# Where two kinds of weights wait: pooled weights two to a raw tile, and the last gate rows in two half-size tiles

## The chip, the cores and the metric

The kernel runs on one core of a Trainium2 chip. The metric is the time of one execution on the device in microseconds (us); a run's time is given as the median over repeated executions. Five engines work side by side: TensorE (PE in the profile; its weight loads are listed as PEld), VectorE (DVE), ScalarE (ACT), GpSimd (POOL) and SyncE (SP). In this kernel GpSimd does next to nothing, and SyncE only issues DMA transfers.

## The reference

The reference is one layer of an encoder block over 1024 tokens of width 1024 in float32: a SwiGLU feed-forward part, a mixing part, a second SwiGLU part and a final norm. The mixing part is where the change lies:

```python
q, k, v, g_ret, p, gates = split(u @ w_in)
ret = retention(rotary(q), rotary(k), v)          # 4 heads of 256
ret = per_head_rms(ret) * silu(g_ret)
pool_out = multiscale_pool(p, pool_w, pool_scale) # 4 groups: (mean - token) @ pool_w[g]
gate = sigmoid(gates + gate_bias)                 # two branches
merged = gate[0] * (ret @ w_ret_up) + gate[1] * (pool_out @ w_pool_up)
h = h + merged @ w_out
```

Each of the four pooling groups has a matrix `pool_w[g]` of 256x256. `w_pool_up` is 1024x1024.

## The kernel before, in words

Activations lie transposed: 128 features on the partitions, 1024 tokens along the row, so a matrix of 1024x1024 is eight tiles. Every float32 operand of a matmul is split into a high part (ScalarE's cast, line 161) and a low part (VectorE's subtraction, line 162; lines 165 and 166 for a split that also scales), and each product takes three matmuls: high by high, high by low, low by high (lines 181 to 183, and 711 to 714 in the plain products). Most large products use Strassen's scheme with seven products of half-size blocks; the products of the pooled branch are plain.

The work is a list of steps, each a preparation (loads, combinations and splits of weights) and a body (the matmuls and what follows them). `Flow.run` issues the preparation of a step four steps ahead of its body, and after each body a few items of background work. This source order is a priority: the framework that builds the program places each instruction as its operands and tiles become free, so the order on an engine can differ from the source's. Instructions under `soon()` get a high priority. SyncE issues its DMAs strictly in the order so found: one that waits holds up those behind it.

The tiles in on-chip memory come from pools by tag:

- `raw`: 4 tiles of 128x1024 float32 (4 KB on each partition, 512 KB in all), for weights as they come from memory, and for some rows.
- `c2`: 8 tiles of 128x512, for combinations of weight blocks (`ru0S` and so on), differences, and sums on their way.
- `wt`: 5 tiles that hold split weights; `mv`: 28 tiles for split activations and some rows; `tl` (4) and `t4` (9) for other rows.

A tile is free for its next user when its last reader is done; if that reader is a store, when the store has landed.

The sequence around the change, in the source's order:

1. The projections' last groups, g2 and g3, use the raw tiles in pairs (`ra`, `rb`).
2. The retention: eight units, and between their steps the pooled branch as filler. First `pool(n)` for the four groups (lines 1379 to 1405): it loads the group's pooled rows (`pl`, two raw tiles for groups 2 and 3; those of groups 0 and 1 have other tiles), loads the block `pool_w[n]` of 128x512 into the first half of a raw tile (`pw`), and splits it. Its products `px` are scaled and split into `po`, which become operands of the next part.
3. `pool_up` (lines 1407 to 1423): for each of the eight tiles mt, the weights `pu0raw` to `pu7raw` (one raw tile each), split in two parts, and the gate rows `pg` (one raw tile each, loaded from `gates`). When the products `pu0d` to `pu7d` are done, VectorE multiplies them onto the gate rows (line 1419), and the result is stored from the same raw tile to `pm`.
4. The merge: groups `ru0` to `ru3` (Strassen groups, prepared two by two), whose weights come in two raw tiles each, `ru0ra`, `ru0rb`, `ru1ra`, `ru1rb` and so on. `combine` (line 455) forms S1 and S2 from them in c2 tiles, line 468 forms S3 in place, line 472 S4. Their results are multiplied by gate rows `rg` (line 1749) and added to the stored `pm` rows (line 1750). Then come the groups `wo0` to `wo3` of the output projection.

So four raw tiles are passed on from `pl` and `pw` to `pu` and `pg` and then to `ru`. All DMAs named here are issued by SyncE (line 140, the helper `load`).

Of the kernel before, what the change touches and what calls it, by code (L numbers as in the profile page):

```python
# [15 lines left out]
ADD, SUB, MUL = ALU.add, ALU.subtract, ALU.mult  # L16
# [4 lines left out]
KT = D // P  # L21
# [69 lines left out]
def block_kernel(ctx: ExitStack, tc, x, x_tok, vecs, f1_in, f1_out, w_in, w_v, pool_w, w_ret, w_pool, w_o,  # L91
# [3 lines left out]
    tt = nc.vector.tensor_tensor  # L95
# [12 lines left out]
    def mv(name):  # L108
        return sb.tile([P, 2, H], F32R, tag="mv", bufs=N_MV, name=name)

    def wt(name, at=0):

        w = sb.tile([P, S + LINE], F32R, tag="wt", bufs=N_WT, name=name)
        return w[:, at : at + S].rearrange("p (z i c) -> p z i c", z=2, i=4)
# [5 lines left out]
    def raw(name):  # L120
        return sb.tile([P, S], F32, tag="raw", bufs=N_RAW, name=name)
# [7 lines left out]
    def c2(name):  # L129
        return sb.tile([P, H], F32, tag="c2", bufs=N_C2, name=name)  # L130
# [8 lines left out]
    def load(dst, src):  # L139
        nc.sync.dma_start(dst, src)  # L140
# [5 lines left out]
    def spill(name, n, width=S):  # L146
        return [dr.tile([P, width], F32, tag=f"{name}{i}", name=f"{name}{i}") for i in range(n)]

    def half(t, j):
        return t[:, j * H : (j + 1) * H]  # L150
# [6 lines left out]
    def flat(w, j, n=4):  # L157
        return w[:, j, :n].rearrange("p a b -> p (a b)")

    def split(hi, lo, src):  # L160
        copy(hi, src)  # L161
        tt(lo, src, hi.bitcast(F32), SUB)  # L162

    def split_scaled(hi, lo, src, by):
        act(hi, src, AF.Copy, scale=by)
        stt(lo, src, by, hi.bitcast(F32), MUL, SUB)

    def operand(src, name):
        m = mv(name)
        split(m[:, 0], m[:, 1], src)  # L170
        return m

    def weights(src, name, at=0):
        w = wt(name, at)
        n = src.shape[-1] // P
        split(flat(w, 0, n), flat(w, 1, n), src)
        return w

    def mm3(dst, w, m, start, stop):

        mm(dst, w[0], m[0], start=start, stop=False, skip_group_check=True)  # L181
        mm(dst, w[0], m[1], start=False, stop=False, skip_group_check=True)  # L182
        mm(dst, w[1], m[0], start=False, stop=stop, skip_group_check=True)  # L183

    def parts(m, at=slice(None)):
        return m[:, 0, at], m[:, 1, at]
# [503 lines left out]
    def plain(M, nk, src, name, evac, begin, banks):  # L690

        t = {}
        for q in range(0, nk, 4):

            def prep(q=q):
                if q == 0:
                    t["raw"] = raw(f"{name}raw")
                    load(t["raw"][:, : nk * P], src)
                t[q] = weights(t["raw"][:, q * P : (q + 4) * P], f"{name}w{q}")
                if q + 4 == nk:  # L700
                    begin()

            def body(q=q):
                if q == 0:
                    t["dst"] = [f(f"{name}d{j}") for j, f in enumerate(banks)]
                for i in range(4):
                    w = parts(t[q], i)
                    m = [parts(M(q + i)[j]) for j in range(2)]
                    first, final = q + i == 0, q + i == nk - 1
                    for j in range(2):  # L710
                        mm(t["dst"][j], w[0], m[j][0], start=first, stop=False)
                        mm(t["dst"][j], w[0], m[j][1], start=False, stop=False)
                    for j in range(2):
                        mm(t["dst"][j], w[1], m[j][0], start=False, stop=final)
                if q + 4 == nk:
                    evac(t["dst"])

            yield prep, body
# [396 lines left out]
    gates = spill("gt", 2 * KT)  # L1115
    pm, ret = spill("pm", KT), spill("ret", KT)
# [16 lines left out]
    def await_stored(*names):  # L1133
        flow.until(lambda: stored.issuperset(names))
# [236 lines left out]
    def pooled_rows(n, i, first=False):  # L1371

        await_stored(f"p{n}")
        name = f"pl{n}{i}"
        r = wide(name) if first else raw(name)
        load(r, pooled[2 * n + i])
        early[n, i] = [operand(half(r, j), f"{name}{j}") for j in range(2)]

    def pool(n):
        Mg, w = {}, []  # L1380

        def prep():
            for i in range(2):
                if (n, i) not in early:
                    pooled_rows(n, i)
                Mg[i] = early[n, i]
            r = raw(f"pw{n}")
            load(half(r, 0), pool_w[n])
            w.append(weights(half(r, 0), f"pw{n}"))

        def body():
            for i in range(2):
                mt = 2 * n + i
                dst = [f(f"px{mt}{j}") for j, f in enumerate((sum_bank, bank))]
                for kt in range(2):
                    for j in range(2):
                        mm3(dst[j], parts(w[0], 2 * kt + i), parts(Mg[kt][j]), kt == 0, kt == 1)
                M[mt] = []
                for j in range(2):
                    m = mv(f"po{mt}{j}")  # L1400
                    with soon():
                        split_scaled(m[:, 0], m[:, 1], dst[j], vec[:, V_SCALE + mt : V_SCALE + mt + 1])
                    M[mt].append(m)

        return prep, body

    def pool_up():
        gate = {}
        for mt in range(KT):

            def begin(mt=mt):
                gate[mt] = raw(f"pg{mt}")
                await_stored(f"t{(KT + mt) // 2}")
                load(gate[mt], gates[KT + mt])

            def evac(dst, mt=mt):
                gt = gate.pop(mt)
                for j in range(2):
                    tt(half(gt, j), dst[j], half(gt, j), MUL)
                load(pm[mt], gt)  # L1420

            yield from plain(M.get, KT, w_pool[mt], f"pu{mt}", evac, begin,
                             (sum_bank, sum_bank if mt < 4 else bank))

    def fillers():

        for n in range(4):
            yield pool(n)
        yield from pool_up()
# [560 lines left out]
```

## Time and profile before

| what | value |
|---|---|
| median of 3 runs | 2144.27 us (2141.74 to 2145.18) |
| the profiled execution's own time | 2143.71 us |
| its span, first to last instruction | 2141.8 us |
| granted TensorE clock, mean | 1.000 |
| moved by DMA | 313.59 MB, mean 146 GB/s |
| the four loads of `pw` (256 KB each) | 2.6 / 3.5 / 4.7 us to landing (least, median, most) |
| the eight loads and eight stores of `pg` (512 KB each) | 2.6 / 3.7 / 6.8 us to landing |

How to read it: every instruction has its line in the kernel, engine, operation, and the tiles that it writes and reads, without buffer numbers (`pg<-pu7d,pg` writes pg from pu7d and pg). A bracket `[1.94 <-DVE ru1wS L162]` says that the engine stood idle for 1.94 us before the instruction, and what ended the wait. In a row of windows stand the stretch, its length, then for PE, PEld, DVE, ACT and POOL the busy time with the number of instructions, the granted clock, the DMA engines' busy share, and GB/s. Matmuls overlap: one takes 0.39 us and the next begins 0.23 us later.

### The profile page before, as it was taken

Reading aid. Unit: us, or ns where it says so; the run is one execution under the profiler, and the core shown is the slowest. Engines: PE = TensorE matmul, PEld = TensorE weight load, DVE = VectorE, ACT = ScalarE, POOL = GpSimd, SP = SyncE. Lnnn points to the kernel's source line nnn. Section 1 sums busy time; section 2 is a strip of 40 time slices with the busy share of each in tenths; the row PEclk is TensorE's granted clock in tenths of the full one; section 3 lists DMA queues with packets and bytes.
Section 4 is the critical chain, followed back from the end, with each engine's and each line's share of the span. In section 5 each row is a group of like instructions: output and inputs, shape, how many; then the busy total and the mean of one; then the engine's idle time right before and its main releaser. Section 6 shows DMA issues by size and latency. Waiting matters only on the chain.

```text
span 2141.8 us, 30121 instructions
## 1 busy us (share of the span) xinstructions
PE 2129.9 (99%) x10798; PEld 1809.6 (84%) x10798; DVE 1874.0 (87%) x3352; ACT 1103.3 (52%) x2082; POOL 0.2 (0%) x4
## 2 busy tenths in 40 slices
PE   9999999999999999999999999999999999999998
PEld 7888888888888888888888998788888888888887
DVE  8798898997986799999988888899988978899796
ACT  8544444554644544544457753456644544455454
POOL 0000000000000000000000000000000000000000
PEclk9999999999999999999999999999999999999999
DMA  7232323585543333233336567624133232358542
GB/s 259 75 133 74 138 84 130 200 275 178 173 142 94 109 121 115 106 122 109 119 128 227 196 203 262 220 89 163 64 105 117 90 123 84 131 199 275 192 138 99
DMA packets 116101, 313.59 MB, mean 146 GB/s; under 512 B 12784, under 2 KB 17008, under 8 KB 115952
## 3 DMA queue, kind: packets, MB, share of 16 engines
q1 hardware_dynamic: 115376, 310.63, 42.6%
q8 instruction: 84, 1.38, 0.3%
q10 hardware_dynamic: 576, 1.05, 0.1%
q14 instruction: 65, 0.53, 0.1%
HBM read 220.93 MB, written 90.70 MB: 145 GB/s over the span
## 4 chain that ended last, share of the span: by engine, by line
PE 91%; DVE 6%; DMA 1%; ACT 1%; issue 1%; SPq 0%; ACTq 0%; DVEq 0%
PE a_b L181 2%; PE a_b L182 2%; PE a_b L183 2%; PE c_b L181 2%; PE c_b L182 2%; PE c_b L183 2%; PE c_e L182 2%; PE c_e L181 2%; PE c_e L183 2%; PE a_e L181 2%; PE a_e L182 2%; PE a_e L183 2%; PE a_a L181 1%; PE a_a L183 1%; PE a_a L182 1%; PE c_a L181 1%
## 5 line engine op out<-in xcount | busy, mean ns | idle before, releaser
L182 PE MATMUL c_b<-n3T,c_wS 128*128 128x512 f32 x176 | 68.6, 390 | 0.0
L183 PE MATMUL c_b<-n3T,c_wS 128*128 128x512 f32 x176 | 68.5, 389 | 0.0
L181 PE MATMUL c_b<-n3T,c_wS 128*128 128x512 f32 x176 | 68.4, 390 | 0.0
L182 PE MATMUL a_b<-n1T,a_wS 128*128 128x512 f32 x168 | 65.4, 389 | 0.0
L181 PE MATMUL a_b<-n1T,a_wS 128*128 128x512 f32 x168 | 65.4, 389 | 0.0
L183 PE MATMUL a_b<-n1T,a_wS 128*128 128x512 f32 x168 | 65.3, 389 | 0.0
L181 PE MATMUL a_a<-n1R,a_wL 128*128 128x512 f32 x120 | 46.7, 389 | 0.0
L182 PE MATMUL a_a<-n1R,a_wL 128*128 128x512 f32 x120 | 46.7, 389 | 0.0
L183 PE MATMUL a_a<-n1R,a_wL 128*128 128x512 f32 x120 | 46.7, 389 | 0.0
L182 PE MATMUL c_a<-n3R,c_wL 128*128 128x512 f32 x112 | 43.6, 389 | 0.0
L181 PE MATMUL c_a<-n3R,c_wL 128*128 128x512 f32 x112 | 43.6, 389 | 0.0
L183 PE MATMUL c_a<-n3R,c_wL 128*128 128x512 f32 x112 | 43.6, 389 | 0.0
L183 PEld LDWEIGHTS c_b<-n3T,c_wS 128*128 128x128 f32 x176 | 33.0, 188 | 6.9
L182 PEld LDWEIGHTS c_b<-n3T,c_wS 128*128 128x128 f32 x176 | 33.0, 188 | 6.8 <-DVE n3T L162 0.2
L181 PEld LDWEIGHTS c_b<-n3T,c_wS 128*128 128x128 f32 x176 | 32.9, 188 | 6.9 <-ACT n3T L161 0.3
L162 DVE TENSOR_TENSOR a_wS<-a_S,a_wS 128x512 fp32r<-128x512 f32 x45 | 31.2, 695 | 8.0 <-ACT a_wS L161 8.0
L183 PEld LDWEIGHTS a_b<-n1T,a_wS 128*128 128x128 f32 x168 | 31.5, 188 | 6.6
L181 PEld LDWEIGHTS a_b<-n1T,a_wS 128*128 128x128 f32 x168 | 31.5, 188 | 6.4
L182 PEld LDWEIGHTS a_b<-n1T,a_wS 128*128 128x128 f32 x168 | 31.5, 188 | 6.4
L182 PE MATMUL c_e<-n3T,c_wL 128*128 128x512 f32 x88 | 34.5, 394 | 0.0
L161 ACT CAST c_wS<-c_S 128x512 fp32r<-128x512 f32 x46 | 28.0, 626 | 12.7 <-DVE c_S L455 7.1
L181 PE MATMUL c_e<-n3T,c_wS 128*128 128x512 f32 x88 | 34.4, 391 | 0.0
(3385 smaller groups left out, 8168.5 us busy)
## 6 DMA issues: line engine op xcount, KB each, us to landing
c_ra<-in_f_in SPq DMA_DIRECT2D x22, 512.0 KB, 3.7
c_rb<-in_f_in SPq DMA_DIRECT2D x22, 512.0 KB, 3.7
a_ra<-in_f_in SPq DMA_DIRECT2D x21, 512.0 KB, 3.8
a_rb<-in_f_in SPq DMA_DIRECT2D x21, 512.0 KB, 3.8
t<-au SPq DMA_DIRECT2D x11, 512.0 KB, 2.9
b<-ag SPq DMA_DIRECT2D x11, 512.0 KB, 4.1
r<-au SPq DMA_DIRECT2D x11, 512.0 KB, 3.8
bra<-in_f_out SPq DMA_DIRECT2D x11, 512.0 KB, 5.9
```

Of the source, the lines that this page charges most:

```text
L161: copy(hi, src)
L162: tt(lo, src, hi.bitcast(F32), SUB)
L181: mm(dst, w[0], m[0], start=start, stop=False, skip_group_check=True)
L182: mm(dst, w[0], m[1], start=False, stop=False, skip_group_check=True)
L183: mm(dst, w[1], m[0], start=False, stop=stop, skip_group_check=True)
```

## The change

In `pool`, every even group now takes one raw tile for two blocks: it loads `pool_w[n]` into its first half and `pool_w[n + 1]` into its second; the odd group splits the second half and loads nothing. In `pool_up`, tiles 0 to 6 work as before. For the last, mt = 7, the gate rows lie in two c2 tiles of 512 columns: two loads instead of one, the same two multiplies, and two stores of half a row instead of one. In all there are three raw tiles fewer in the sequence (two of `pw`, one of `pg`) and two c2 tiles more; the number of DMAs rises by two; matmuls, casts and VectorE operations are the same in number and size.

```diff
--- before.py
+++ after.py
@@ -1376,6 +1376,8 @@
         load(r, pooled[2 * n + i])
         early[n, i] = [operand(half(r, j), f"{name}{j}") for j in range(2)]
 
+    blocks = {}
+
     def pool(n):
         Mg, w = {}, []
 
@@ -1384,9 +1386,11 @@
                 if (n, i) not in early:
                     pooled_rows(n, i)
                 Mg[i] = early[n, i]
-            r = raw(f"pw{n}")
-            load(half(r, 0), pool_w[n])
-            w.append(weights(half(r, 0), f"pw{n}"))
+            if n % 2 == 0:
+                r = blocks["pw"] = raw(f"pw{n}")
+                for j in range(2):
+                    load(half(r, j), pool_w[n + j])
+            w.append(weights(half(blocks["pw"], n % 2), f"pw{n}"))
 
         def body():
             for i in range(2):
@@ -1405,19 +1409,27 @@
         return prep, body
 
     def pool_up():
-        gate = {}
+        gate, stores = {}, {}
         for mt in range(KT):
 
             def begin(mt=mt):
-                gate[mt] = raw(f"pg{mt}")
                 await_stored(f"t{(KT + mt) // 2}")
-                load(gate[mt], gates[KT + mt])
+                if mt < KT - 1:
+                    r = raw(f"pg{mt}")
+                    load(r, gates[KT + mt])
+                    gate[mt] = [half(r, j) for j in range(2)]
+                    stores[mt] = [(pm[mt], r)]
+                    return
+                gate[mt] = [c2(f"pg{mt}{j}") for j in range(2)]
+                for j, g in enumerate(gate[mt]):
+                    load(g, half(gates[KT + mt], j))
+                stores[mt] = [(half(pm[mt], j), g) for j, g in enumerate(gate[mt])]
 
             def evac(dst, mt=mt):
-                gt = gate.pop(mt)
-                for j in range(2):
-                    tt(half(gt, j), dst[j], half(gt, j), MUL)
-                load(pm[mt], gt)
+                for j, g in enumerate(gate.pop(mt)):
+                    tt(g, dst[j], g, MUL)
+                for to, at in stores.pop(mt):
+                    load(to, at)
 
             yield from plain(M.get, KT, w_pool[mt], f"pu{mt}", evac, begin,
                              (sum_bank, sum_bank if mt < 4 else bank))
```

## The prediction

> **What bounds the kernel now.** I read the page first, the first two lines of busy times, to see whether any engine has time to give away.
>
> ```profile
> span 2141.8 us, 30121 instructions
> PE 2129.9 (99%) x10798; PEld 1809.6 (84%) x10798; DVE 1874.0 (87%) x3352; ACT 1103.3 (52%) x2082; POOL 0.2 (0%) x4
> ```
>
> TensorE is busy for 2129.9 of 2141.8 us. The change takes no matmul away, so by this line it can win at most the 11.9 us in which TensorE stood still. Next come the stretches: the busy time of each engine in windows chosen around the places where TensorE's share dips. The second column is the length, the third TensorE's busy time.
>
> ```profile
> 0.00:50.00 50.00, 47.85 (x201) 36.80 (x202) 44.07 (x72) 42.92 (x77) 0.20 (x4) 1.00 0.71 255
> 1140.00:1180.00 40.00, 39.61 (x257) 35.18 (x256) 38.99 (x72) 32.77 (x66) 0.00 (x0) 1.00 0.67 219
> 1260.00:1300.00 40.00, 39.79 (x264) 35.96 (x263) 39.62 (x85) 21.06 (x52) 0.00 (x0) 1.00 0.47 141
> 1356.00:1372.00 16.00, 14.06 (x62) 11.30 (x61) 13.55 (x23) 7.34 (x13) 0.00 (x0) 1.00 0.82 308
> 1420.00:1500.00 80.00, 79.41 (x348) 64.83 (x347) 78.78 (x129) 47.05 (x83) 0.00 (x0) 1.00 0.39 136
> 1500.00:2000.00 500.00, 499.63 (x2577) 427.02 (x2577) 447.15 (x798) 249.92 (x464) 0.00 (x0) 1.00 0.40 135
> 2100.00:2141.80 41.80, 35.64 (x161) 29.02 (x159) 24.55 (x59) 16.30 (x34) 0.00 (x0) 0.99 0.26 101
> ```
>
> Of the 11.9 us, the start has 2.15 and the tail 6.16, and the change touches neither. About 3.6 us are left between 50 and 2100 us: 0.39, 0.21, 1.94, 0.59, 0.37, and under 0.1 elsewhere. One of these is more than half of it, and it lies at 1356 to 1372 us, where the last pooled tile (pu7) has just ended and the merge (groups ru0 and ru1) begins. The list of TensorE's waits names it:
>
> ```profile
> PE ru1b L183 <- DVE ru1wS L162: 1.9, 1, 1.9
> PE wo0e L183 <- DVE wo0wS L162: 0.4, 1, 0.4
> ```
>
> The chain of waits, followed back from that matmul, shows what was late (start, duration, what):
>
> ```profile
> 1353.04 1.21 DVE pg L1419 x2
> 1354.27 2.59 DMA pm<-pg
> 1356.88 5.65 DMA ru1rb<-in_w_ret
> ...
> 1362.55 0.70 DVE ru1S L455
> ...
> 1366.88 0.70 DVE ru1wS L162
> 1367.62 0.50 PE ru1b L183
> ```
>
> This is the whole case. VectorE multiplies pu7's sums by the gate rows in raw tile pg7. The product is stored (2.59 us), and only when the store has landed may the raw tile be used again: the second half of group ru1's weights is loaded into it (issued 1356.88, 0.02 us after the landing). From the load come ru1's combination and its split, and TensorE waits 1.94 us for the split's low part. The gate rows of pu7 hold the raw tile that ru1 needs, and the change puts exactly these rows elsewhere.
>
> **Part 1: the last gate rows in two c2 tiles.** It removes one raw tile, one 512 KB load and one 512 KB store; it adds two 256 KB loads and two 256 KB stores. The two multiplies are the same. To see when ru1's second half could be loaded, take the SyncE queue (start, issue time):
>
> ```profile
> 1328.80 0.41 SPq L140 DMA_DIRECT2D pg<-gt  x1
> ...
> 1333.20 0.32 SPq L140 DMA_DIRECT2D pm<-pg  x1
> 1333.61 0.38 SPq L140 DMA_DIRECT2D ru0ra<-in_w_ret  x1
> ...
> 1337.05 0.33 SPq L140 DMA_DIRECT2D ru0rb<-in_w_ret  x1
> ...
> 1342.84 0.32 SPq L140 DMA_DIRECT2D pm<-pg  x1
> 1345.52 0.33 SPq L140 DMA_DIRECT2D ru1ra<-in_w_ret  x1
> ```
>
> There are four raw tiles. At 1328.80 pg7 takes the one that came free; pg5, pg6 and pu7's weights hold the others. The four loads of ru0 and ru1 then follow the releases: ru0ra after pu7's weights are split, ru0rb after pg5's store (1333.20), ru1ra after pg6's store (1342.84, 2.68 us earlier), ru1rb after pg7's. With pg7 out of the pool each load moves up one release: ru0ra takes the tile that pg7 took, and ru1rb gets the one that ru1ra has now. So ru1rb should be issued at about 1345.5 instead of 1356.88, 11.4 us sooner, and with the same 5.65 us it has landed by 1351.2. From landing to TensorE's matmul the chain now takes 1367.62 - 1362.55 = 5.07 us, which gives 1356.3 at best. TensorE wants the split 1.94 us before 1367.62, at 1365.7. The margin is 9.4 us, so the wait goes as a whole unless most of the gain in the load is lost again.
>
> What could be late next at the same place? The split needs one of five weight buffers, and it is the sixth split of the merge, so it waits for the first product of ru0 to end, which is when ru1's first begins:
>
> ```profile
> 1354.19 0.39 PE L181 MATMUL ru1a<-ruR,ru1wL 128*128 128x512 f32 x1
> ```
>
> That is still 11 us ahead of 1365.7. So the wait of 1.94 us is worth 1.94, if nothing behind it gives it back.
>
> Issues: SyncE makes two more, at the 0.32 us of a row above 0.64 us in all, the load's share at a place where nothing waits (pu7's multiply is 24 us behind the load at 1328.80). The extra store stands behind the last multiply; queued behind it are the merge's loads of pm rows and ru2's weights, which come a third of a microsecond later. The merge's last groups read pm7, so a later landing costs nothing soon. I take 0 for all of these; the bounds are -0.1 (two halves start sooner than one whole) and +0.3 (one issue on the path).
>
> The price elsewhere: two of the eight c2 tiles are taken from the load until the stores land, about 1357. Combinations of ru0 and ru1 and the differences of the retention rows share them. Four differences, two tiles of pg7 and two combinations of ru0 make eight, just full. A combination of ru1 that had to wait for pg7's store would start at 1356.88 rather than 1362.55, still 5.67 us sooner than now, against the 1.94 needed. So I take 0 here, too, with +0.3 as the upper end.
>
> **Part 2: the pooled weights two to a raw tile.** Four loads of 256 KB remain four; two raw tiles are saved. pw1 and pw3 are issued right behind pw0 and pw2, so they move up; each tile is held until the second block's split. Raw rows of the pooled groups (pl) and the first weights of pu can then be loaded sooner. The stretch in which this happens, in windows of 10 us:
>
> ```profile
> 1150.00:1160.00 10.00, 9.96 (x74) 9.26 (x73) 9.92 (x20) 6.48 (x12) 0.00 (x0) 1.00 0.79 261
> 1160.00:1170.00 10.00, 9.65 (x48) 7.41 (x47) 9.60 (x20) 8.51 (x17) 0.00 (x0) 1.00 0.63 226
> 1170.00:1180.00 10.00, 10.00 (x71) 9.31 (x70) 9.91 (x17) 9.77 (x23) 0.00 (x0) 1.00 0.80 256
> ```
>
> TensorE loses 0.39 us here. So the best that part 2 can do by itself is -0.39. VectorE (fourth pair of numbers) is busy for 9.6 to 9.9 of every 10 us: data that land sooner meet a VectorE that has no hole for them, and I count no gain. What an operation costs if it is put ahead of one that TensorE waits for is the row of the splits, 0.69 us:
>
> ```profile
> L162 DVE TENSOR_TENSOR pl<-pl,pl x16: 682/690/695, 1134.6 to 1190.3; 128x512 fp32r<-128x512 f32 x16
> L162 DVE TENSOR_TENSOR pw<-pw,pw x4: 685/686/687, 1159.1 to 1191.5; 128x512 fp32r<-128x512 f32 x4
> ```
>
> For part 2 I take 0, between -0.39 and +4.8 (the last rival).
>
> **What stands behind the gain.** TensorE comes 1.94 us sooner to the merge, where VectorE is full:
>
> ```profile
> 1370.00:1380.00 10.00, 10.00 (x45) 8.28 (x45) 4.23 (x7) 3.94 (x7) 0.00 (x0) 1.00 0.75 244
> 1400.00:1410.00 10.00, 10.00 (x46) 8.29 (x45) 10.00 (x17) 4.75 (x9) 0.00 (x0) 1.00 0.01 2
> 1390.57 0.69 DVE L1750 TENSOR_TENSOR ru<-ru,ru0h 128x512 f32<-128x512 f32 x1
> 1392.03 0.69 DVE L1749 TENSOR_TENSOR ru1h<-ru1b,rg 128x512 f32<-128x512 f32 x1 [0.77 <-PE ru1b L183]
> ```
>
> The full stretch starts at 1392.03 with a wait of 0.77 us for TensorE's ru1b, and VectorE had 5.77 us free at 1370 to 1380. A TensorE that is 1.94 us sooner therefore starts the full stretch sooner, and the splits of ru1 that stand at 1362 to 1372 now can move into earlier gaps. I count the whole 1.94 as kept.
>
> **The sum.** The profiled execution took 2143.71 us, 1.9 outside its span of 2141.8; the median of the three runs is 2144.27, 0.56 above it. Sum: -1.94 + 0 + 0 gives 2141.8 for that execution and 2142.3 for the median. With the small bounds (-0.1 to +0.6) and the other mid-kernel waits, the case's own range is 2140.7 (all 3.57 us gone) to 2142.9. A change of 0.2% is 4.3 us, about what a measurement of this kernel can tell from none; this gain is 0.09%.
>
> **Rivals.** *VectorE gives part of it back.* If at 1392 VectorE can start only 0.77 us sooner, the rest turns up at the next product that waits for it, wo0e, whose 0.4 us become 1.6. Then 0.77 are won: 2143.5. For it speaks VectorE's full 10.00; against it the gap of 5.77 us before.
>
> *The change does not free ru1rb.* SyncE issues in order. If the load of ru1rb stays behind pg7's stores in the queue, it starts at 1354.27 + 0.65 = 1354.9, 1.96 us sooner than now, which is just the wait; behind the wait for their landing it is no sooner at all, and 2144.3 stays.
>
> *Earlier loads fill a full VectorE (slower).* Place: 1150 to 1200 us. Raw tiles that come free sooner let the splits of one pl tile (2), of pw3 (1) and of pu0 and pu1 (4) be queued ahead of the pooled sums' splits, for which TensorE waits. Seven at 0.69 are 4.8 us; less 1.94, 2.9 us slower, 2147.2; half of them give 2144.7. It decides from three operations on (1.94 / 0.69 = 2.8). For it: VectorE at 9.9 of 10. Against it: the sums' splits are marked as urgent, and TensorE's losses are 0.39 us now.
> By the Trainium skill (TensorE: Matmul & The Clock Gate, "What's actually happening") an idle window of about 3.4 us halves TensorE's clock until a busy one has passed; as an estimate from that page, a single wait of 4.8 us would cost some 1.7 us more, 2148.9. The trace's longest wait in the kernel's middle, 1.94 us, left the granted clock at 1.00 (row 1356 to 1372); no run here shows a longer one there.
>
> *TensorE's busy time hides waits (faster by over 0.2%).* If short waits lay inside busy rows, the 3.57 us would be no bound. It would take 2.4 us beyond the 1.94, or 5 ns on each of the some 450 matmuls of 100 us around the merge. The rows speak against it: 45 matmuls in 10 us with VectorE at 4.23, 46 with VectorE at 10.00.
> The Trainium skill (Perfetto Trace Analysis, "Identifying the Most-Contended Engine") calls matmul busy time no good measure of the distance to the limit and takes that of the weight loads; here that is 84%, and by it there would be room. The trace shows the same 8.28 and 8.29 of 10 in both rows, so the room is not one of waits.
>
> **Numbers.** Forecast (2142.3) 0.55; VectorE gives back 0.17; not freed 0.04; earlier loads 0.20, of which 0.10 beyond 0.2%; hidden waits 0.04. So faster 0.04, slower 0.10, the same 0.86. The range reaches from 2140.3 (the floor of 2140.7 with the noise of a median) to 2147.2, the full price of the slower rival.
>
> **What would show it.** Right: ru1rb issued at about 1345 and before pg7's stores; no wait of TensorE at ru1b; TensorE's idle time in the middle down from 3.6 to about 1.6 us; VectorE's full stretch starting some 2 us sooner. Wrong: a new wait at px, pu or wo products of the size of the old one, or a load of pg7 that comes late because c2 tiles are short.

## The result, and the profile after

| | median, us | lowest to highest, us | runs |
|---|---|---|---|
| before, run beside it | 2142.31 | 2140.84 to 2146.28 | 22 |
| changed kernel | 2140.11 | 2139.80 to 2141.11 | 22 |

The ratio is 0.9986 (95% interval 0.9981 to 0.9992): the change is faster by 0.14%, less than the 0.2% from which the prediction speaks of a change. The medians differ by 2.20 us, where 1.94 was forecast; yet 2140.11 lies 0.2 us under the range on record, because the forecast of 2142.3 started from a median of 2144.27 for the kernel before, and over more runs that median is 2142.3. What also changed is the spread: 5.4 us before, 1.3 us after.

The profiled execution of the changed kernel took 2140.30 us. The page's first lines, to be held against those of before:

```profile
span 2138.5 us, 30135 instructions
PE 2129.7 (100%) x10798; PEld 1809.8 (85%) x10798; DVE 1874.0 (88%) x3352; ACT 1100.8 (51%) x2082; POOL 0.2 (0%) x4
```

The same work on every engine, and 8.8 us of idle TensorE instead of 11.9. Not all of these 3.1 us belong to the change: in the first 50 us TensorE is busy for 48.79 us instead of 47.85, in a stretch that no edit touches and in which it stands idle for 1.2 to 2.3 us in the profiles of this case, edited kernels and unedited ones alike. The stretches in windows, in the columns known from before:

```profile
1140.00:1180.00 40.00, 39.31 (x254) 34.90 (x253) 38.66 (x71) 32.58 (x67) 0.00 (x0) 1.00 0.66 217
...
1356.00:1372.00 16.00, 16.00 (x73) 13.23 (x72) 15.45 (x27) 7.83 (x14) 0.00 (x0) 1.00 0.72 242
...
1500.00:2000.00 500.00, 500.00 (x2582) 427.57 (x2581) 447.77 (x798) 249.72 (x464) 0.00 (x0) 1.00 0.40 136
```

At 1356 to 1372 us the 1.94 us are gone to nothing. At 1140 to 1180 TensorE loses 0.69 instead of 0.39, and the 0.37 of the second feed-forward part (1500 to 2000) are gone, too. The list of TensorE's waits no longer has a line for ru1b; the first of these two lines is as before, the second is new (before, TensorE waited 0.2 us at px, for VectorE's po):

```profile
PE wo0e L183 <- DVE wo0wS L162: 0.4, 1, 0.4
PE px L181 <- DVE g3A L1158: 0.4, 1, 0.4
```

The SyncE queue shows why:

```profile
1322.91 0.94 SPq L140 DMA_DIRECT2D pg<-gt  x2
1324.83 0.33 SPq L140 DMA_DIRECT2D ru0ra<-in_w_ret  x1
...
1344.96 0.32 SPq L140 DMA_DIRECT2D pm<-pg  x1
...
1348.76 0.33 SPq L140 DMA_DIRECT2D ru1rb<-in_w_ret  x1
1355.20 0.92 SPq L140 DMA_DIRECT2D pm<-pg  x2
```

ru1's second half is now issued at 1348.76, ahead of pg7's stores (1355.20) and behind pg6's (1344.96), as the step said; it had been 1356.88. And VectorE's full stretch begins 2.17 us sooner, with the same short wait in front:

```profile
1389.86 0.69 DVE L1761 TENSOR_TENSOR ru1h<-ru1b,rg 128x512 f32<-128x512 f32 x1 [0.77 <-PE ru1b L183]
```

### The profile page after: what moved, and what is told of

Same layout as the page of the kernel before. It is cut to its first block, busy times and chain, and to the rows that moved or that the text cites. A ratio compares the mean times of both kernels' runs of the same rounds, so it can differ in the third digit from the quotient of the medians.

```text
span 2138.5 us, 30135 instructions
## 1 busy us (share of the span) xinstructions
PE 2129.7 (100%) x10798; PEld 1809.8 (85%) x10798; DVE 1874.0 (88%) x3352; ACT 1100.8 (51%) x2082; POOL 0.2 (0%) x4
## 4 chain that ended last, share of the span: by engine, by line
PE 93%; DVE 5%; ACT 1%; issue 1%; DMA 1%; SPq 0%; ACTq 0%; DVEq 0%
PE c_b L181 2%; PE c_b L182 2%; PE c_b L183 2%; PE a_b L181 2%; PE a_b L183 2%; PE a_b L182 2%; PE c_e L182 2%; PE c_e L181 2%; PE c_e L183 2%; PE a_e L181 2%; PE a_e L182 2%; PE a_e L183 2%; PE a_a L181 1%; PE a_a L183 1%; PE a_a L182 1%; PE c_a L181 1%
```

## The experiments

Two questions were open: which part of the change carries the gain, and why the kernel before spreads over more than 5 us. All "before" medians beside the runs are 2141.7 to 2142.5 us.

**The gate rows alone.** `pool` is left as before; only `pool_up` is changed.

> The kernel before with the last gate rows in two c2 tiles and nothing else (each pooled block keeps its own raw tile). Theory A (the raw tile of pg7 is what TensorE waited for): the wait at ru1b goes from 1.94 us to 0, ru1's second half is issued ahead of pg7's stores, and the time falls by all of the change's gain, about 2.2 us (2.0 to 2.6). Theory B (all three saved raw tiles count): the wait shrinks but stays over 0.5 us, and the gain is 0.5 to 1.5 us. Theory C (the spread of the kernel before, 2140.8 to 2146.3 us over 22 runs, comes from a DMA on TensorE's path, which only ru1's late load is): the runs of this kernel lie within 1.5 us of each other.

Measured: 2139.86 us against 2142.32 (ratio 0.9987, 0.9978 to 0.9996), runs 2139.48 to 2141.38; no wait at ru1b, the load issued at 1350.11 and pg7's stores at 1356.46. The whole gain comes with this half of the edit: theory A holds, B falls. The runs lie within 1.9 us, where C had expected 1.5.

**The blocks in pairs alone.** `pool` is changed; pg7 stays in a raw tile.

> The kernel before with the pooled blocks two to a raw tile and nothing else (pg7 stays in a raw tile). Theory A: ru1's second half still follows pg7's store, the wait at ru1b stays at 1.9 us (1.4 to 2.5), and the time is that of the kernel before within 0.4 us; if anything slower by the 0.3 us that TensorE loses at the pooled products in the changed kernel. Theory B: a gain of 0.5 to 1.5 us. Theory C: the runs spread over 3 us or more, as those of the kernel before.

Measured: 2142.47 us against 2142.32 (0.9999, 0.9990 to 1.0008), runs 2140.72 to 2144.66. No gain, and the spread stays, as A and C have it. But the wait at ru1b was smaller than the 1.4 to 2.5 us expected:

```profile
PE ru1b L183 <- DVE ru1wS L162: 0.8, 1, 0.8
```

```profile
L140 SPq DMA_DIRECT2D ru1rb<-in_w_ret x1: 333/333/333, 1357.3 to 1357.3; - x1
...
DMA to landing us min/median/max: 3.9/3.9/3.9
```

The load was issued no sooner, but took 3.9 us where the first profile had 5.65. This points to the length of the wait as a matter of how long this one transfer takes; two profiles alone do not show it.

**Both last gates in c2 tiles.** In the changed kernel, `mt < KT - 1` becomes `mt < KT - 2`.

> The changed kernel with the gate rows of the last two pooled tiles (pg6 and pg7) in four c2 tiles. Theory A: the raw tiles are no longer short, so nothing more is won: the changed kernel's time within 0.4 us, ru1's first half issued earlier, at about 1333 us. A c2 pool that is short (half of its eight tiles held) would show as a new wait of TensorE of 0.5 us or more at the first merge products, and as that much more time.

Measured: 2140.34 us (0.9990, 0.9981 to 0.9999), 0.2 above the changed kernel; ru1's halves issued at 1334.87 and 1341.00, and no wait at the merge. Nothing more is to be won with raw tiles, and four of eight c2 tiles held cost nothing there.

**The other end of the same wait.** pg7 stays in its raw tile, and ru1's second half goes elsewhere:

```diff
-            ra, rb = raw(f"{name}ra"), raw(f"{name}rb")
+            if name == "ru1":
+                low = [c2(f"{name}rb{j}") for j in range(2)]
+                for j, r in enumerate(low):
+                    load(r, half(wb, j))
```

> The kernel before, with pg7 in its raw tile and each pooled block in its own, but with the second half of ru1's weights in two c2 tiles instead of a raw tile. Theory A: the load no longer waits for pg7's store, is issued before 1350 us, and the wait at ru1b goes: 2.0 us faster than before, less what two c2 tiles held until about 1374 us cost (0 to 1 us). Theory D (the gain comes from another order of the instructions, not from the raw tile): no gain, or a wait of 1 us or more elsewhere.

Measured: 2140.39 us (0.9989, 0.9980 to 0.9998), no wait at ru1b, the loads issued from 1321.68 on. The same gain from another edit with another order of instructions: it is the raw tile between pg7 and ru1 that makes the wait, and theory D falls.

**The disputed load twice, with the wait and without.** One line in `blocks()`, in the kernel before and in the one with the gate rows alone:

```diff
             load(rb, wb)
+            if name == "ru1":
+                load(rb, wb)
```

> The kernel before, in which the second half of ru1's weights is loaded twice into the same raw tile (the same data; the second load waits for the first to land). Theory A with C (TensorE waits on this load and on nothing else there, so any microsecond of it is a microsecond of the kernel): the second load adds one landing, 3.4 to 5.7 us, and the wait at ru1b grows from 1.9 to 5 to 8 us; the time grows by 3 to 6 us. Rival (VectorE, full behind it, would have held TensorE there anyway): the wait grows, but the time by under 2 us, since a later wait shrinks in turn.

> The kernel with the last gate rows in two c2 tiles and nothing else, in which the second half of ru1's weights is loaded twice in the same way. Theory A with the prediction's margin of some 9 us: the second load lands at about 1358 us instead of 1353.9, the chain to TensorE takes 5.1 us, TensorE needs it at about 1365.5, so the wait at ru1b is under 0.5 us and the time that of the kernel with the gate rows alone within 0.5 us. If the margin were used up: a wait of 2 us or more and as much more time.

Measured in the kernel before: 2148.36 us against 2142.45 (1.0026, 1.0015 to 1.0038), 5.9 us slower. Its chain of waits:

```profile
1356.27 4.10 DMA ru1rb<-in_w_ret
...
1360.43 5.60 DMA ru1rb<-in_w_ret
...
1366.06 0.70 DVE ru1S L457
```

The data land 3.5 us later than in the first profile of before. The waits at ru1b are 3.2 and 0.2 us. That is 1.5 more than the 1.94 there, and less than the 5 to 8 us expected. What else is lost at this place is the clock, which neither theory had:

```profile
1368.00:1370.00 2.00, 1.77 (x4) 1.16 (x4) 2.00 (x5) 1.19 (x3) 0.00 (x0) 0.50 0.13 45
1370.00:1372.00 2.00, 1.77 (x5) 1.18 (x5) 2.00 (x4) 0.24 (x1) 0.00 (x0) 0.50 0.99 328
1372.00:1374.00 2.00, 2.00 (x6) 1.61 (x5) 1.87 (x4) 1.42 (x3) 0.00 (x0) 0.50 0.83 305
1374.00:1376.00 2.00, 2.00 (x8) 1.58 (x8) 0.31 (x1) 0.93 (x2) 0.00 (x0) 0.81 0.90 356
```

The granted clock stands third from the end, ahead of the DMA share: 0.50 for over 6 us after the wait, which costs some 3.1 us (half of the 5.54 us that TensorE was busy in the first three rows, and a fifth of 2). Together that is 4.6 us; group ru2 begins 4.4 us later than in the first profile of before (1396.2 against 1391.8). This profile was of the fastest of the seven runs (2146.91 us), so what makes up the rest of the median's 5.9 was not seen. The expected size (3 to 6 us) was met, mostly for a reason that was not expected: the wait alone grew by less than the 2 us that the rival allowed. The rival's own sign did not come, though: no later wait shrank, wo0e waits 0.4 us as ever.

With the gate rows in c2 the kernel with the second load took 2140.93 us (0.9991, 0.9982 to 1.0001). That is 1.1 us over the gate rows alone in the first set of runs (2139.86) and 0.6 over them in a later set (2140.33); neither ran beside it, and under 0.5 was expected. The wait at ru1b was 0, so the margin held; the profile shows two others, 0.8 us at px (it comes from a pooled block, below, not from this edit) and this one:

```profile
PE ru1a L181 <- ACT ru1b L494: 0.5, 1, 0.5
```

```profile
1360.09 0.62 ACT L161 CAST ru1wS<-ru1S 128x512 fp32r<-128x512 f32 x1 [3.31 <-DVE ru1S L457]
1360.62 0.58 ACT L494 COPY ru1b<-ru1a 128x512 f32<-128x512 f32 x1
```

ScalarE waited 3.31 us for ru1's combination, and the copy that TensorE needed stood behind it in the queue: here a late operand was paid for by what was queued behind its reader.

**The kernel before, three profiles more.** No edit.

> The kernel before once more, for its profile. Theory C: the landing of ru1's second half and the wait at ru1b differ from profile to profile (landing 3.5 to 7 us, wait 0.5 to 3.5 us), and TensorE's busy time outside that wait is the same; the span follows the wait. Rival: the wait is 1.9 us each time, and what differs lies elsewhere (the start, the tail).

> As the look before this one: the same kernel, a second profile. Theory C: another landing time, another wait, and the two spans differ by the difference of the waits, within 0.7 us for the start and the tail.

> The kernel before, a third extra profile. Theory F (a wait of about 2 us at ru1b is near the length at which TensorE's clock is lowered, so that some executions pay 1.6 us more at half clock and others nothing): a wait of 0.8 to 2.5 us; if the granted clock falls in the 4 us after it, the time is over 2144 us, and otherwise under. Theory C (the landing time alone): the time follows the wait with the clock at 1.00.

Measured: 2146.03, 2143.25 and 2141.51 us. From each profile the time from ru1b's first matmul to ru2a's can be read, a stretch with the same matmuls in every kernel; first the kernel with the gate rows alone, in its second set of runs:

```profile
L181 PE MATMUL ru2a<-ruR,ru2wL x8: 389/389/389, 1389.5 to 1397.0; 128*128 128x512 f32 x8
L181 PE MATMUL ru1b<-ruT,ru1wS x8: 389/389/389, 1365.0 to 1378.0; 128*128 128x512 f32 x8
```

That is 24.5 us, as in every profile of an edited kernel without the wait. The kernel before in its third extra profile, and then in its first:

```profile
L181 PE MATMUL ru2a<-ruR,ru2wL x8: 389/389/389, 1390.2 to 1397.6; 128*128 128x512 f32 x8
L181 PE MATMUL ru1b<-ruT,ru1wS x8: 389/389/397, 1365.4 to 1378.6; 128*128 128x512 f32 x8
```

```profile
L181 PE MATMUL ru2a<-ruR,ru2wL x8: 389/389/389, 1394.7 to 1402.2; 128*128 128x512 f32 x8
L181 PE MATMUL ru1b<-ruT,ru1wS x8: 389/389/628, 1366.4 to 1383.2; 128*128 128x512 f32 x8
```

24.8 and 28.3 us; the profile of the prediction, read the same way, has 26.7, the second extra one 27.0. So one kernel loses between 0.3 and 3.8 us at this place, from one execution to the next:

| profile of before | load issued, us | to landing, us | wait at ru1b, us | clock after it | ru1b to ru2a, us |
|---|---|---|---|---|---|
| third extra | 1356.5 | 4.4 | none listed | 1.00 | 24.8 |
| of the prediction | 1356.9 | 5.6 | 1.9 | 1.00 | 26.7 |
| second extra | 1356.8 | 6.1 | 2.2 | 1.00 | 27.0 |
| first extra | 1359.2 | 4.6 | 2.0 | half for some 3 us | 28.3 |

In the first three the wait follows the landing, as theory C says. The fourth fits as far as the wait goes: its load was issued late, but TensorE, too, came to ru1b 1.3 us later than in the profile of the prediction (1366.4 against 1365.1). For the time theory C fails on it: the clock adds the rest. In 2 us windows of that profile:

```profile
1368.00:1370.00 2.00, 1.07 (x4) 0.87 (x5) 2.00 (x4) 0.78 (x2) 0.00 (x0) 0.90 1.02 413
1370.00:1372.00 2.00, 2.00 (x7) 1.51 (x6) 1.89 (x4) 0.00 (x0) 0.00 (x0) 0.50 1.04 413
1372.00:1374.00 2.00, 2.00 (x8) 1.63 (x7) 0.00 (x0) 0.95 (x2) 0.00 (x0) 0.74 0.54 154
```

The clock is at half after a wait of 2.0 us, and costs 0.20 + 1.00 + 0.52 = 1.7 us. After 1.9 and 2.2 us in the other two profiles it stayed at 1.00, and after 3.2 it fell for 6 us. Theory F fits: a wait of this length was followed by a lower clock in one profile and not in two others. But F was drawn from these profiles, and the third extra one, taken to test it, had none of the 0.8 to 2.5 us of wait that F expected. Only this one profile and that of the doubled load show the clock fall; what decides between the cases was not tried.

**The changed kernel and the gate rows alone, side by side; the pairs cut differently.** The third kernel puts blocks 1 and 2 into one raw tile, and 0 and 3 each into their own.

> The changed kernel once more, beside the kernel with the gate rows alone on the same chip. Theory E (the blocks in pairs trade a variable wait for a fixed one: the load of the third block no longer lands on TensorE's path at 1165 us, where it cost 0.2 to 1.1 us, but its cast now stands ahead of an urgent copy on ScalarE and costs 0.4 us): the median is that of the gate rows alone within 0.4 us, above rather than below it, and no run lies more than 1.5 us over the lowest. Rival (the blocks in pairs are worth as much as the gate rows): 1 us or more below it.

> The kernel with the last gate rows in two c2 tiles and nothing else, once more. Theory E: the lowest runs are 0.2 to 0.4 us under the changed kernel's lowest, the highest above its highest, since the third block's load still lands on TensorE's path; the median is within 0.4 us. Rival: 1 us or more above the changed kernel.

> The changed kernel, in which blocks 1 and 2 share a raw tile and blocks 0 and 3 have one each, so that the third block is loaded at about 1141 us and its cast can stand ahead of the stretch with the urgent copies. Theory E: no wait of ScalarE for the third block, TensorE's loss at 1160 to 1170 us down to 0.2 us or less, no run more than 1.5 us over the lowest, and 0.2 to 0.5 us under the changed kernel. Rival (the loss there is a matter of VectorE's full queue): the loss stays at 0.4 us or more, no gain.

Measured: 2140.44, 2140.33 and 2140.31 us; highest runs 2142.51, 2143.89 and 2143.79. The kernel before took 2141.66 in this set, so the gain is 1.2 to 1.4 us here, less than in the sets above, and the intervals just reach no gain (0.9983 to 1.0001, 0.9985 to 1.0003, 0.9984 to 1.0001). The three medians are alike within 0.13 us, as theory E has it, and its rival falls; that no run of the changed kernel or of the third one lies more than 1.5 us over the lowest failed for both. What the pairs trade is seen at 1160 to 1170 us, in TensorE's busy time. The gate rows alone, second set; after it the changed kernel, first profile; last, blocks 1 and 2 together:

```profile
1160.00:1170.00 10.00, 9.65 (x48) 7.36 (x47) 9.61 (x20) 8.46 (x17) 0.00 (x0) 1.00 0.63 232
```

```profile
1160.00:1170.00 10.00, 9.40 (x46) 7.13 (x45) 9.89 (x21) 8.22 (x17) 0.00 (x0) 1.00 0.56 201
```

```profile
1160.00:1170.00 10.00, 10.00 (x58) 8.65 (x58) 9.87 (x21) 8.35 (x17) 0.00 (x0) 1.00 0.79 289
```

With each block in its own tile, ScalarE waits for the third block's landing and TensorE loses 0.2 to 1.1 us, by profile. In pairs 0 and 1, 2 and 3, the load is early, but its cast, still waiting for it, stands ahead of an urgent copy:

```profile
1158.32 0.62 ACT L161 CAST pw<-pw 128x512 fp32r<-128x512 f32 x1 [0.83 <-DMA pw<-in_pool_w]
1158.85 0.36 ACT L599 COPY g3A<-g2x 128x256 f32<-128x256 f32 x1
```

What this costs is not fixed, as theory E had it: in the four profiles with these pairs TensorE loses 0.2 to 0.7 us at 1160 to 1170 us, and 0.2 is from the changed kernel's own second profile. With 1 and 2 together nothing is lost there, and still the median is not the 0.2 to 0.5 us lower that was expected: the profile gives the half microsecond back in the second feed-forward part (387.9 us from its first product to its last against 387.3 to 387.6 in the other edited kernels). No version beats the changed kernel by what can be measured.

## Why the prediction was wrong in its number and right in its mechanism

**The load moves up and the wait goes: right.** The chain of waits of one profile had named the cause, and the kernel with the gate rows alone and the one with ru1 in c2 show it from both ends. The load came 8.1 us sooner, not 11.4. It followed pg6's store, as forecast, but this store moved: it was issued 2.1 us later than before (1344.96 against 1342.84), since VectorE's multiply for it ended later, and it took 3.8 us to land instead of 2.68. The load itself took 3.4 us, not 5.65, and so landed at 1352.2, near the forecast 1351.2: two misses that nearly cancel, which is luck. Counted as in the prediction, 8.4 us of the margin of 9.4 were there.

**c2 tiles at no cost, and VectorE giving nothing back: right.** No wait of the merge appeared even with four tiles held, and VectorE's full stretch moved by 2.17 us. The rivals "gives part of it back" and "not freed" fall.

**The pairs at nothing: right for the median**, which is 0.15 us higher with the pairs than without in the kernel before, and 0.11 with the gate rows in c2, each run side by side. (In a row of windows VectorE is the third pair of numbers, not the fourth; the values that the prediction reads are VectorE's.) The slower rival had its place right and its engine wrong: a load that lands sooner did put work ahead of TensorE's (0.4 us in the first profile), but on ScalarE and for one cast, not for seven operations of VectorE.

**The step that failed is the sum's**: "The profiled execution took 2143.71 us, 1.9 outside its span of 2141.8; the median of the three runs is 2144.27". It took one profile's wait for a constant and a median of three runs for the kernel's time. The three runs (2145.18, 2144.27, 2141.74) already lay 3.4 us apart for one and the same kernel, which asked for a cause. Over the 98 runs of the kernel before that stand beside these kernels, the median is 2142.25, and 31 lie over 2143; over the 88 runs of the five kernels without the wait, in seven sets (the doubled load left out), the median is 2140.21, and 2 lie over 2143. The same sum from 2142.31 gives 2140.37, 0.26 from what was measured, and the floor of the range, taken from the same base, would have come down by the same 2 us. The wait that the prediction priced at 1.94 us is 0 to 2.2, and with the clock up to 3.8. The gain is 2.0 us between these medians. That it lies so near the price in the sum is in part luck: the price varies from execution to execution, and the second feed-forward part, below, adds to the gain.

**The clock: half seen.** The slower rival asked whether a new wait could bring the clock down, and answered from one row that 1.94 us left it at 1.00. The question was not put to the wait that the change removes. The Trainium skill (TensorE: Matmul & The Clock Gate, "What's actually happening") has the clock halved after an idle window of about 3.4 us that runs freely, without regard to the program. The measured fall to 0.50 agrees; that it followed waits of 2.0 and 3.2 us, in neither of which such a window can lie idle as a whole, does not, and the measurement decides.

**Left over.** The kernel before also needs longer in the second feed-forward part, in all four profiles. The rows are for before in the prediction's profile, and then for the gate rows alone:

```profile
L181 PE MATMUL c_a<-n3R,c_wL x112: 389/389/397, 1507.5 to 1888.3; 128*128 128x512 f32 x112
```

```profile
L181 PE MATMUL c_a<-n3R,c_wL x112: 389/389/397, 1505.2 to 1885.1; 128*128 128x512 f32 x112
```

380.8 against 379.9 us; the four profiles of before have 380.6 to 380.8, those of the five kernels without the wait 379.9 to 380.5. TensorE's idle time there is 0.37 us of it, so the rest lies in rows that count as busy, as the rival of hidden waits had it, though far from the 2.4 us that this rival needed. The doubled load in the kernel before, which has the wait at ru1b, does not show it (380.0), so it is no echo of that wait; a different placement of instructions far from the edit is a guess that was not tried. Nor does it make the gain alone: with the blocks in pairs the stretch takes 380.2 us, ru1b still waits, and the median is that of the kernel before. But the third extra profile, with no wait at ru1b, still took 2141.51 us, 1.3 over the median without the wait. So how the 2.0 us divide between the wait, the clock and this stretch stays open.

## What to carry to other kernels

Ask of a buffer that is handed from a store to a load who reads the load's data next: here 512 KB of scratch for one tile's gate rows held up the next stage's weights, and two tiles of a pool with room set them free. A wait for a DMA on the path of the engine that bounds the kernel was not a number here but a spread, so read several profiles before pricing it. A wide set of runs is a hint of such a wait, no more: two kernels without it have a run 4.1 us over their lowest. A few runs of the kernel before are a base only as good as their spread.

## What the runs showed of the hardware that was not expected

A wait of TensorE of 2.0 us was followed in one profile by half clock that cost 1.7 us, while waits of 1.9 and 2.2 us were not; one of 3.2 us was followed by over 6 us at half. The same 512 KB load, issued at the same point of the same program within 0.4 us, landed after 4.4, 5.6 and 6.1 us.
